# Spread VectorE sums, last store on ScalarE, and first products over three row tiles in a one-core MLP kernel

## The chip, the cores and the metric

The kernel runs on one core of one Trainium2 chip. The metric is the device time of one execution in microseconds (us), lower is better. Most kernels were timed in 3 to 9 executions; their medians are quoted. The spread within such a group is 0.3 to 1.7 us, which is as large as the effects discussed here. So the trace of one profiled execution per kernel, whose times are printed to 0.01 us, carries most of the argument, and the medians are used as a check. One trace is one execution, and its start varies: where this matters, all traces of a kind are given.

Names of engines in profile lines: PE is TensorE (matmul), PEld its weight loads, DVE is VectorE, ACT is ScalarE, POOL is GpSimd, SP is SyncE. An engine's name with q is its sequencer, which issues DMAs.

## The reference

```python
# x: 16 x 512 x 768, w1: 768 x 3072, b1: 3072, w2: 3072 x 768, all float32
y = np.matmul(x, w1) + b1
y = 0.5 * y * (1.0 + erf(y / np.sqrt(2.0)))
return np.matmul(y, w2).astype(np.float32)
```

## The kernel before

The 8192 rows go through in blocks of 1024. Both products are done by a Strassen-Winograd scheme: seven products of half-size operands instead of eight, at the price of sums of operands on VectorE (`x_sums` for x, `prep_wt` for a tile of W1) and sums of results. Operands are float16, sums in PSUM are float32. W1 comes in 12 tiles of 256 columns. The first two row blocks share the W1 tiles (units are the pairs of row block and W1 tile listed in `seq`).

The start, before the Strassen units: SyncE loads row tiles 0 to 3 of x (128 rows each) and W1 tile 0 as float32, VectorE casts them, TensorE transposes x, and W1 tiles 0 and 1 are multiplied with the first row block in the plain way. GpSimd loads W1 tile 1, row tiles 4 to 7 and further W1 tiles meanwhile. `spin` is dummy products, meant to keep TensorE's clock up.

```python
for t in range(4):
    nc.sync.dma_start(out=xf[:, t, :], in_=xr[:, t, :])
for half in range(2):
    r = slice(half * KQ, (half + 1) * KQ)
    nc.sync.dma_start(out=wf[:, r, :], in_=w1r[:, r, 0:2 * P])
# ... (identities, GpSimd's loads)
spin(9)
for t in range(4):
    xhs[t] = xh_of(0, t)
    nc.vector.tensor_copy(out=xhs[t], in_=xf[:, t, :])
    transpose_pe(0, t, copy_halves if t == 3 else nc.scalar.copy)
    # ... (b1 transposed at t == 0)
    spin(2)
for r, c in ((slice(0, KQ), slice(0, P)), (slice(0, KQ), slice(P, 2 * P)),
             (slice(KQ, 2 * KQ), slice(0, 2 * P))):
    nc.vector.tensor_copy(out=w1_raw(wts[0])[:, r, c], in_=wf[:, r, c])
# ...
for half in range(2):
    for side in range(2):
        plain(0, 0, side, half)      # W1 tile 0, rows 0 to 511
for side in range(2):
    plain_done(0, 0, side)
plain(1, 0, 0, 0)                    # W1 tile 1
transpose_pe(0, 4)
# ...
```

The sums of the first units. `fill_a(pos, slot)` is called between the products of unit `pos`; `soon` is a list of VectorE work that is done a little at each slot and emptied at the end of a unit. Unit 7 (`at[1, 0]`) is the first on the second row block.

```python
def fill_a(pos, slot):
    # ...
    if pos == at[1, 0] - 2 and slot in (2, 5):
        transpose_pe(1, X1_PE[slot // 3])
    if slot == (1 if pos < at[1, 0] else 4) and pos + 1 < len(seq) and seq[pos + 1][0] == 0:
        prep_wt(seq[pos + 1][1])           # four sums
    if slot == 4:
        if pos in (3, 6):
            prep_wt(pos // 6)              # W1 tiles 0 and 1 for the second block
        # ...
    if slot == 1:
        if pos in (at[1, 0] - 2, at[1, 0] - 1):
            h = pos - at[1, 0] + 2
            x_sums(1, soon, slice(h * RH // 2, (h + 1) * RH // 2))   # four sums
    # ...
```

The end: the last unit stores a 384 KB block (`u.store(0)`), then finishes the last two 128-row pieces one by one (`last`).

```python
def last(self, banks):
    for t in range(2):
        self.mm(4, banks[t], True, 0, self.C, (t,))
        o = self.dst[:, 1, t, 0, :]
        tt(o, banks[t][:, t * N4:(t + 1) * N4], o, ADD)
        nc.sync.dma_start(out=orr[:, self.sb * 8 + 2 + t, N2:N2 + N4], in_=o)
```

## Time and profile before

| what | value |
|---|---|
| time | 853.23 us, median of 3 (853.05 to 853.4) |
| profiled span | 851.5 us |
| TensorE busy | 844.9 us, 99% |
| VectorE busy | 667.0 us, 78% |

TensorE is the limit: a kernel of this kind can only gain where TensorE waits or does dummy work. The list of waits has three lines for it, 2.6 us in all (columns: engine and what it wrote, then the releaser; us in total, times, longest).

```profile
PE bX L738 <- DVE arena L724: 1.2, 1, 1.2
PE bT L311 <- DVE arena L744: 1.2, 2, 0.9
PE bY L386 <- ACT bY L604: 0.2, 1, 0.2
```

Where the time stands at the start is read from the timeline of TensorE (columns: start us, length us, engine, line, operation, output <- input, shape, count; in brackets the idle time before it and what ended it).

```profile
9.01 0.51 PE L311 MATMUL bT<-ident,arena 128*128 128x128 f16 x6 [0.93 <-DVE arena L744]
...
10.09 0.81 PE L760 MATMUL bX<-arena 128*128 128x512 f16 x3
...
12.67 0.81 PE L760 MATMUL bX<-arena 128*128 128x512 f16 x3
13.32 0.50 PE L311 MATMUL bT<-ident,arena 128*128 128x128 f16 x6
```

The line at 9.01 is the transposes of row tile 3. They wait for VectorE's cast of this tile, which starts when the tile has landed:

```profile
8.04 0.91 DVE L744 CAST arena<-arena 128x768 f16<-128x768 f32 x1 [0.96 <-DMA arena<-in_x_dram]
```

At 10.09 the first real product starts; at 12.67 W1 tile 0 is done and tile 1 begins. I call this moment S. At 13.32 row tile 4 is transposed.

The stretch around 40 us, by windows that each hold one unit (columns: window, its length, busy us and number of instructions of PE, PEld, DVE, ACT and POOL, granted clock, share of the DMA engines, GB/s):

```profile
28.32:32.85 4.53, 4.53 (x22) 2.06 (x21) 4.25 (x12) 3.32 (x5) 0.00 (x0) 1.00 1.23 194
32.85:38.05 5.20, 5.20 (x34) 2.72 (x33) 3.57 (x8) 4.00 (x6) 0.00 (x0) 1.00 1.34 194
38.05:42.92 4.87, 4.70 (x25) 2.06 (x22) 4.70 (x11) 4.00 (x6) 0.00 (x0) 1.00 1.11 279
42.92:47.84 4.92, 4.78 (x23) 2.04 (x22) 4.61 (x11) 3.37 (x6) 0.00 (x0) 1.00 1.02 413
```

A unit of 21 products takes 4.53 us when nothing disturbs it. The second line holds two sets of six transposes, 0.34 us each, so it is not late. The third and fourth are late by 0.34 and 0.39 us, with VectorE busy nearly throughout.

The chain of waits says where the lateness came from (start us, length us, what; the lines left out are issue times and more work of VectorE):

```profile
13.25 11.00 DMA arena<-in_x_dram
...
24.53 11.75 DMA arena<-in_w_dram
...
36.31 0.37 DVE arena L191
...
46.46 0.69 DVE arena L611
...
47.19 0.81 PE bY L386 x3
```

Up to 47 us the kernel was paced by a chain of GpSimd's loads that ends with W1 tile 6 landing at 36.28 (24.53 + 11.75), then by VectorE's backlog from there.

### The profile page before, as it was taken

The numbers are of one execution on the slowest core, as the hardware profiler recorded it, in microseconds if no ns is written. First come the engines' busy times: TensorE is split into PE (matmuls) and PEld (weight loads), VectorE is DVE, ScalarE is ACT, GpSimd is POOL, SyncE is SP. The second block draws the span as 40 slices with busy tenths as digits, with TensorE's granted clock in tenths as the row PEclk, the third lists the DMA queues.
The fourth block names the chain that finished last, engine by engine and source line by source line (L and its number), as shares of the span: only waits on it lengthen the run. The fifth ranks groups of instructions, "written<-read, shape, count | busy, mean of one in ns | idle before, by whom it ended". The sixth has DMA issues, their size and how long they took to land.

```text
span 851.5 us, 16488 instructions
## 1 busy us (share of the span) xinstructions
PE 844.9 (99%) x6432; PEld 568.8 (67%) x6432; DVE 667.0 (78%) x1128; ACT 420.9 (49%) x686; POOL 83.3 (10%) x135
## 2 busy tenths in 40 slices
PE   8999999999999999999999999999999999999998
PEld 5444445687544897448974499645995469944798
DVE  4866678786657998579976799668996689956998
ACT  4777762122277512784138722477216771267611
POOL 5021100002100002000020000200002100010000
PEclk9999999999999999999999999999999999999999
DMA  9996986749999599987999689994999969984398
GB/s 227 213 256 89 253 169 244 267 184 221 212 340 226 186 326 372 304 183 233 334 368 292 141 283 335 360 294 113 312 335 355 277 128 325 347 322 172 100 298 295
DMA packets 143522, 219.05 MB, mean 257 GB/s; under 512 B 61756, under 2 KB 84724, under 8 KB 143444
## 3 DMA queue, kind: packets, MB, share of 16 engines
q1 hardware_dynamic: 117968, 179.83, 66.8%
q0 software_dynamic: 25440, 38.15, 20.7%
q8 instruction: 50, 0.82, 0.4%
q14 instruction: 28, 0.23, 0.1%
q10 hardware_dynamic: 36, 0.01, 0.0%
HBM read 180.30 MB, written 47.87 MB: 268 GB/s over the span
## 4 chain that ended last, share of the span: by engine, by line
PE 94%; DMA 4%; DVE 1%; ACT 0%; issue 0%; POOL 0%; DVEq 0%; ACTq 0%
PE bY L386 20%; PE bY L491 15%; PE bX L386 13%; PE bX L491 10%; PE bW L386 7%; PE bZ L386 7%; PE bZ L491 5%; PE bW L491 5%; PE bY L430 5%; DMA arena<-in_x_dram 3%; PE bZ L430 2%; PE bX L430 2%; PE bW L430 2%; DMA arena<-in_w_dram 1%; PE bY L578 1%; DVE arena L191 1%
## 5 line engine op out<-in xcount | busy, mean ns | idle before, releaser
L191 DVE TENSOR_TENSOR arena<-arena 128x1536 f16<-128x1536 f16 (+7 forms) x632 | 402.9, 668 | 7.8 <-DMA arena<-arena 1.6
L386 PEld LDWEIGHTS <-arena 128*128 128x128 f16 x1974 | 192.5, 98 | 224.7 <-issue 1.1
L491 PEld LDWEIGHTS <-arena 128*128 128x128 f16 x3528 | 292.1, 98 | 8.3 <-issue 0.4
L386 PE MATMUL bY<-arena 128*128 128x512 f16 x846 | 214.5, 379 | 0.3 <-ACT bY L604 0.2
L611 DVE TENSOR_TENSOR arena<-bY,arena 128x512 f32<-128x512 f32 (+1 forms) x102 | 69.3, 680 | 126.3 <-PE bY L386 87.6
L491 PE MATMUL bY<-arena 128*128 128x192 f16 x1500 | 138.3, 246 | 0.0
L386 PE MATMUL bX<-arena 128*128 128x512 f16 x564 | 138.2, 379 | 0.0
L604 ACT COPY bY<-bX 128x512 f32<-128x512 f32 (+1 forms) x143 | 78.6, 550 | 119.3 <-DVE arena L540 81.9
L402 ACT ACTIVATE arena<-arena,b1t 128x1024 f16<-128x1024 f32 x94 | 108.0, 1149 | 54.4 <-DVE arena L639 54.4
L624 ACT COPY arena<-bW 128x512 f32<-128x512 f32 (+1 forms) x147 | 81.0, 551 | 91.0 <-PE bW L491 43.9
L491 PE MATMUL bX<-arena 128*128 128x192 f16 x1020 | 93.1, 246 | 0.1
L639 DVE TENSOR_TENSOR arena<-bZ,arena 128x512 f32<-128x512 f32 (+1 forms) x102 | 69.2, 679 | 20.7 <-PE bZ L386 17.9
L386 PE MATMUL bZ<-arena 128*128 128x512 f16 x282 | 76.2, 379 | 0.0
L386 PE MATMUL bW<-arena 128*128 128x512 f16 x282 | 76.2, 379 | 0.0
L430 PEld LDWEIGHTS <-arena 128*128 128x128 f16 x528 | 51.6, 98 | 34.1 <-issue 0.2
L523 POOL DMA_DIRECT2D out_dram<-arena x42 | 30.5, 728 | 404.8 <-DVE arena L635 368.2
L407 ACT ACTIVATE arena<-bX,b1t 128x512 f16<-128x512 f32 x94 | 64.0, 681 | 10.0 <-PE bX L386 10.0
L407 ACT ACTIVATE arena<-bY,b1t 128x512 f16<-128x512 f32 x94 | 63.3, 673 | 0.0
L655 ACT COPY bZ<-bY 128x512 f32<-128x512 f32 (+1 forms) x54 | 29.0, 537 | 65.9 <-DVE arena L639 33.7
L297 POOL DMA_DIRECT2D arena<-in_x_dram x60 | 32.3, 544 | 250.8 <-DMA arena<-arena 141.3
L491 PE MATMUL bZ<-arena 128*128 128x192 f16 x504 | 48.5, 246 | 0.0
L491 PE MATMUL bW<-arena 128*128 128x192 f16 x504 | 48.5, 246 | 0.0
(60 smaller groups left out, 398.9 us busy)
## 6 DMA issues: line engine op xcount, KB each, us to landing
arena<-w2s SPq DMA_DIRECT2D x294, 288.0 KB, 4.6
arena<-w1s SPq DMA_DIRECT2D x72, 672.0 KB, 7.1
out_dram<-arena POOLq DMA_DIRECT2D x42, 384.0 KB, 7.2
w2s<-arena SPq DMA_DIRECT2D x49, 288.0 KB, 3.7
arena<-in_x_dram POOLq DMA_DIRECT2D x60, 192.0 KB, 7.3
w1s<-arena SPq DMA_DIRECT2D x12, 672.0 KB, 6.6
arena<-in_w_dram POOLq DMA_DIRECT2D x17, 384.0 KB, 7.4
out_dram<-arena SPq DMA_DIRECT2D x17, 384.0 KB, 3.3
```

The lines of the kernel that those rows point to most:

```text
L191: nc.vector.tensor_tensor(out=o, in0=a, in1=b, op=op)
L297: nc.gpsimd.dma_start(out=xhs[t], in_=xr[:, sb * 8 + t, :])
L386: nc.tensor.matmul(out=dst[:, 0:RH], lhsT=w1_op(self.wt, slot)[:, c, :], rhs=a[:, c, :], start=first and c == 0, stop=c == self.C - 1, ski ...
L402: nc.scalar.activation(out=self.G[1][:, hi, :, :], in_=self.tmp, func=GELU, bias=b1t[:, 2 * hi + 1:2 * hi + 2])
L407: nc.scalar.activation(out=self.G[0][:, hi, row, :], in_=bank[:, 0:RH], func=GELU, bias=b1t[:, 2 * hi:2 * hi + 1])
L430: nc.tensor.matmul(out=dst[:, 0:N2], lhsT=a, rhs=w[:, :, c, :], start=first and c == 0, stop=c == self.C - 1, skip_group_check=True)
L491: nc.tensor.matmul(out=dst[:, t * N4:(t + 1) * N4], lhsT=a, rhs=w[:, c, :], start=first and c == 0 and t == ts[0], stop=c == NQ - 1, skip_ ...
L523: eng.dma_start(out=orr[:, s0:s0 + 2, right * N2:(right + 1) * N2], in_=self.dst[:, r].rearrange("p t h n -> p t (h n)"))
L604: nc.scalar.copy(out=bY[u.g % 2][:, 0:u.F], in_=bX[u.g % 2][:, 0:u.F])
L611: nc.vector.tensor_tensor(out=u.c22(), in0=bY[u.g % 2][:, 0:u.F], in1=w[:, 0:u.F], op=ADD)
L624: nc.scalar.copy(out=w[:, 0:u.F], in_=bW[:, 0:u.F])
L639: nc.vector.tensor_tensor(out=u.c12(), in0=bZ[:, 0:u.F], in1=w[:, 0:u.F], op=ADD)
```

## The change: intent and diff

Three parts. First, take VectorE's sums out of the crowded units 5 to 7: three of the four sums of W1 tiles 0 and 1 are done in idle time near the start, and the second x block's sums and second transpose are spread over more units. Second, let ScalarE issue the last store so that it needn't queue behind SyncE's issue. Third, start the products earlier: load W1 tile 0 ahead of row tile 3, multiply the first three row tiles, and do row tile 3 afterwards.

```diff
-        def prep_wt(n):
+        def prep_wt(n, ks=()):
             o = {s: w1_op(wts[n], s) for s in range(7)}
-            for d, a, b in ((T3, B22, T1), (T1, T1, B11), (T2, B22, T1), (T4, B21, T2)):
-                later(KQ * P, lambda d=d, a=a, b=b: tt(o[d], o[a], o[b], SUB), soon)
+            early = ((T3, B22, T1, SUB), (T2, T3, B11, ADD), (T4, B21, T2, SUB), (T1, T1, B11, SUB))
+            usual = ((T3, B22, T1, SUB), (T1, T1, B11, SUB), (T2, B22, T1, SUB), (T4, B21, T2, SUB))
+            for d, a, b, op in [early[k] for k in ks] if ks else usual:
+                later(KQ * P, lambda d=d, a=a, b=b, op=op: tt(o[d], o[a], o[b], op), soon)
@@ the last stores
-                    nc.sync.dma_start(out=orr[:, self.sb * 8 + 2 + t, N2:N2 + N4], in_=o)
+                    (nc.sync, nc.scalar)[t].dma_start(out=orr[:, self.sb * 8 + 2 + t, N2:N2 + N4], in_=o)
@@ the start
-        for t in range(4):
+        for t in range(3):
             nc.sync.dma_start(out=xf[:, t, :], in_=xr[:, t, :])
         ...
             nc.sync.dma_start(out=wf[:, r, :], in_=w1r[:, r, 0:2 * P])
+        nc.sync.dma_start(out=xf[:, 3, :], in_=xr[:, 3, :])
@@
-        for t in range(4):
+        for t in range(3):
             xhs[t] = xh_of(0, t)
             nc.vector.tensor_copy(out=xhs[t], in_=xf[:, t, :])
-            transpose_pe(0, t, copy_halves if t == 3 else nc.scalar.copy)
+            transpose_pe(0, t)
             ...
-            spin(2)
+            spin((2, 2, 4)[t])
@@
+        first, rest = slice(0, 3 * P), slice(3 * P, RH)
+        plain(0, 0, 0, 0, first)
+        plain(0, 0, 1, 0, first)
+        xhs[3] = xh_of(0, 3)
+        nc.vector.tensor_copy(out=xhs[3], in_=xf[:, 3, :])
+        transpose_pe(0, 3, nc.vector.tensor_copy)
+        plain(0, 0, 0, 1, first)
+        plain(0, 0, 1, 1, first)
+        prep_wt(0, range(3))
+        flush(soon)
         for half in range(2):
             for side in range(2):
-                plain(0, 0, side, half)
+                plain(0, 0, side, half, rest)
         for side in range(2):
             plain_done(0, 0, side)
+        prep_wt(1, range(3))
+        flush(soon)
@@ fill_a: second transpose, x sums, W1 sums
+        X1_AT = ((5, 2), (6, 1))
-            if pos == at[1, 0] - 2 and slot in (2, 5):
-                transpose_pe(1, X1_PE[slot // 3])
+            if (pos, slot) in X1_AT:
+                transpose_pe(1, X1_PE[X1_AT.index((pos, slot))])
+            if pos == at[1, 0] - 1 and slot == 2:
+                x_sums(1, soon, slice(RH // 2, RH), (0, 1))
-                if pos in (3, 6):
-                    prep_wt(pos // 6)
+                if pos in (3, 4):
+                    prep_wt(pos - 3, (3,))
-                if pos in (at[1, 0] - 2, at[1, 0] - 1):
-                    h = pos - at[1, 0] + 2
-                    x_sums(1, soon, slice(h * RH // 2, (h + 1) * RH // 2))
+                if pos == at[1, 0] - 2:
+                    x_sums(1, soon, slice(0, RH // 2), (0, 1))
+                if pos == at[1, 0]:
+                    x_sums(1, soon, ks=(2, 3))
... (W1 tiles are stored back to DRAM at earlier units, table KEEP)
```

More of the change, by code (lines that the diff above doesn't have):

```diff
@@ L303, in transpose_dma @@
             nc.sync.dma_start_transpose(out=xT_of(sb, t), in_=xhs[t])
-        def copy_halves(out, in_):
-            for c in (slice(0, KQ), slice(KQ, 2 * KQ)):
-                nc.scalar.copy(out=out[:, c, :], in_=in_[:, c, :])
         def transpose_pe(sb, t, copy=nc.scalar.copy):
@@ L839 @@
         X1_PE = (3, 7)
+        X1_AT = ((5, 2), (6, 1))
+        KEEP = {at[1, 0]: range(7), at[0, 7] + 1: (7,), at[0, 8]: (8,), at[0, 9]: (9,), at[0, 10]: (10,), at[0, 11]: (11,)}
         def transposes_a(pos):
@@ L881, in fill_a @@
                     transposes_a(pos)
-                for n in {at[1, 0]: (0, 2, 3, 4, 6, 5), at[1, 1]: (1,)}.get(
-                        pos, seq[pos][1:] if pos > at[1, 6] and seq[pos][0] and seq[pos][1] > 6 else ()):
+                for n in KEEP.get(pos, ()):
                     keep(n)
```

## The prediction

> What bounds the kernel now. The page gives TensorE 844.9 of 851.5 us busy (99%), the chain of waits is 94% TensorE, and the list of waits has 2.6 us for it in all. In the steady first phase a unit of 21 matmuls of 512 columns takes 4.53 us, 216 ns each. So only three places can give anything: the start, a stretch about 40 us in, and the tail.
>
> 1. Start. The timeline has the first real product at 10.09 us. It waits for row tile 3: landed at 8.0, cast until 8.95, transposed from 9.01, copied by ScalarE from 9.56. W1 tile 0 lands at about 9.1 and 10.1. From 10.09 to 12.67 TensorE runs tile 0's twelve products without a gap. With the change W1's first half should land near 7.8, so six 384-column products start near 8.5 (row tile 2 is copied at 8.49) and last 1 us. Then TensorE, in order, waits for row tile 3, now the last of the same six transfers: landing 9.7 to 10.1, cast 0.56, transposes 0.34, second-half products 0.97, the 128-column rest 0.65: end at 12.3 to 12.7 against 12.67. The 1.6 us won at the first product is mostly given back as a wait for row tile 3. It is capped too: row tiles 4, 5, 6 land at about 12.9, 13.9, 14.9 (DMA view) and are transposed at 13.32, 14.30, 15.29, so a gain over 0.4 us would turn into waits there. Splitting costs little: the Trainium skill ("TensorE: Matmul & The Clock Gate", Part 1) gives a matmul N columns at 2.4 GHz plus about 2.5 ns; the trace agrees (216 ns for 512, 56 for 128), so twelve more cost 0.03 us. The same page lets the clock fall only after about 3.4 us idle; the idle 0.93 us at 8.1 to 9.0 did not lower it here. I expect -0.25 us (0 to -0.4).
>
> 2. Sums. In the windows, the units at 38.70 and 43.57 last 4.87 and 4.92 us, 0.34 and 0.39 over 4.53, with VectorE busy 4.70 and 4.71: sums of W1 tiles 0, 1 and 6 and of the second x block fall on three units, and VectorE starts them late, waiting until 36.31 for W1 tile 6. The 5.20 us of the unit at 33.50 are two transposes (2 x 0.34), which stay. The change puts six W1 sums (0.37 each) into idle VectorE time at 10.7 to 14.9, two into earlier units, and two big x sums one unit later. I count about 4.4, 2.9 and 3.8 us of VectorE then, all under 4.53; the second transposed copy (0.80 on ScalarE) moves too. I expect -0.65 us of the 0.73. The stores of W1 tiles move earlier; TensorE waits in neither place: 0.
>
> 3. Tail. The last VectorE sum ends near 848.27; SyncE issues the two last stores back to back, 847.97 to 848.97, about 0.5 us each. On ScalarE the second can start at 848.3: -0.15 us.
>
> Sum: 853.23 - 0.25 - 0.65 - 0.15 = 852.2 us; range 851.6 to 853.0. Chances: faster by over 2% 0, within 2% 0.99, slower 0.01.
>
> What would show it: first product near 8.5, then a wait of about 1 us at row tile 3's transposes, row tile 4's transposes at 12.95 to 13.3; units near 38 and 43 at 4.53 (4.87 with a transpose); last store issued 0.2 us earlier; TensorE unchanged between.
>
> What would make it wrong: row tile 3 landing after 10.2; W1 tile 1 landing late, with its sums now before VectorE's transposed copies; the wait for W1 tile 6 still pushing VectorE behind.

## The result, and the profile after

The change measured 852.75 us (median of 6, 852.64 to 853.0) against 853.16 us (median of 6, 853.0 to 853.53) of the kernel before in the same rounds. The ratio is 0.9995 with a 95% interval of 0.9982 to 1.0008. Ratios here and below are the mean time of one kernel's fast runs over that of the other's of the same rounds, so not quite the ratio of the medians quoted. The time lies in the predicted range, but the gain is about 0.4 us, not 1.05, so the parts have to be looked at one by one.

TensorE's timeline of the start, after the change:

```profile
8.96 0.66 PE L759 MATMUL bX<-arena 128*128 128x384 f16 x3 [0.77 <-DVE arena L751]
9.46 0.65 PE L759 MATMUL bY<-arena 128*128 128x384 f16 x3
11.00 0.51 PE L309 MATMUL bT<-ident,arena 128*128 128x128 f16 x6 [0.88 <-DVE arena L773]
11.34 0.65 PE L759 MATMUL bX<-arena 128*128 128x384 f16 x3
...
12.99 0.81 PE L759 MATMUL bX<-arena 128*128 128x512 f16 x3
13.63 0.50 PE L309 MATMUL bT<-ident,arena 128*128 128x128 f16 x6
```

The first product starts 1.13 us earlier than before (8.96 against 10.09). After six products TensorE then waits for the cast of row tile 3 (the wait of 0.88 us at 11.00):

```profile
10.38 0.56 DVE L773 CAST arena<-arena 128x768 f16<-128x768 f32 x1 [0.37 <-DMA arena<-in_x_dram]
```

W1 tile 1 begins at S = 12.99, which is 0.32 us later than before.

The units around 40 us, again one window for each:

```profile
33.16:38.03 4.87, 4.87 (x28) 2.39 (x27) 3.38 (x9) 4.00 (x6) 0.00 (x0) 1.00 1.63 182
38.03:43.04 5.01, 5.01 (x28) 2.39 (x27) 3.62 (x8) 4.00 (x6) 0.00 (x0) 1.00 0.99 225
43.04:47.57 4.53, 4.53 (x22) 2.05 (x21) 3.74 (x7) 3.43 (x6) 0.00 (x0) 1.00 1.01 418
```

Two units now hold one set of transposes each, so 4.87 is undisturbed for them. What is left is 0.14 us in the second of these; VectorE is down from 4.7 and 4.6 us to 3.6 and 3.7.

The chain of waits now runs through row tile 3 and then stays on TensorE:

```profile
3.14 7.22 DMA arena<-in_x_dram
10.38 0.57 DVE arena L773
11.00 0.51 PE bT L309 x6
11.51 0.49 PE bX L759 x3
```

The GpSimd loads and VectorE's backlog have left the chain; the load of row tile 3 has come onto it.

The tail. First the issues of the last stores on SyncE, before and then after, with ScalarE's one after:

```profile
847.50 0.37 SPq L523 DMA_DIRECT2D out_dram<-arena  x1
847.97 1.00 SPq L502 DMA_DIRECT2D out_dram<-arena  x2
```

```profile
847.20 0.37 SPq L521 DMA_DIRECT2D out_dram<-arena  x1
847.66 0.44 SPq L500 DMA_DIRECT2D out_dram<-arena  x1
847.99 0.38 ACTq L500 DMA_DIRECT2D out_dram<-arena  x1
```

TensorE ends at E = 847.88 before and 847.57 after (end of the last entry on TensorE in the chain). The last issue is over 1.09 us after E before the change (848.97), and 0.80 us after E with it (848.37). So the issue did come 0.3 us earlier. The span does not show it: the end comes 3.61 us after E before (851.487) and 3.66 us after E with the change (851.232). Pages print spans to 0.1 us only; here and below they are taken from the traces, which hold them to 0.001 us.

With a fourth mark, the start M of the six products on the tile bX with which TensorE goes over to unit 8 (47.84 before, 47.57 after), the span splits into four stretches. This table is used for all experiments; its entries are differences of times read from the traces.

| kernel | S | S to M | M to E | E to end |
|---|---|---|---|---|
| before | 12.67 | 35.17 | 800.04 | 3.61 |
| after | 12.99 | 34.58 | 800.00 | 3.66 |
| difference | +0.32 | -0.59 | -0.04 | +0.05 |

The sum is -0.26 us, the difference of the two profiled spans. So the sums gave what was hoped, the new start cost, and the tail gave nothing. M to E is 799.9 to 800.1 us in every kernel, which bounds what the moved stores of the W1 tiles can have done there. They were not undone alone; before M they are not needed, since the x sums without them (below) reach the lowest S to M that any trace shows.

### The profile page after: what moved, and what is told of

Its sections match the earlier page's. It is cut to its first block, busy times and chain, and to the rows that moved or that the text cites. A ratio compares the mean times of both kernels' runs of the same rounds, so it can differ in the third digit from the quotient of the medians.

```text
span 851.2 us, 16509 instructions
## 1 busy us (share of the span) xinstructions
PE 844.6 (99%) x6444; PEld 569.6 (67%) x6444; DVE 667.6 (78%) x1127; ACT 419.9 (49%) x684; POOL 83.4 (10%) x135
## 4 chain that ended last, share of the span: by engine, by line
PE 98%; DMA 1%; SPq 0%; DVE 0%; issue 0%
PE bY L384 21%; PE bY L489 15%; PE bX L384 14%; PE bX L489 10%; PE bZ L384 7%; PE bW L384 7%; PE bZ L489 5%; PE bW L489 5%; PE bY L428 5%; PE bZ L428 2%; PE bX L428 2%; PE bW L428 2%; PE bY L576 1%; DMA arena<-in_x_dram 1%; PE bX L576 1%; PE bX L759 0%
## 5 line engine op out<-in xcount | busy, mean ns | idle before, releaser
L191 DVE TENSOR_TENSOR arena<-arena 128x768 f16<-128x768 f16 (+4 forms) x630 | 403.4, 671 | 8.0 <-DMA arena<-arena 2.0
L609 DVE TENSOR_TENSOR arena<-bY,arena 128x512 f32<-128x512 f32 (+1 forms) x102 | 69.4, 681 | 127.1 <-PE bY L384 89.4
```

Of the source, the lines that this page charges most:

```text
L191: nc.vector.tensor_tensor(out=o, in0=a, in1=b, op=op)
L609: nc.vector.tensor_tensor(out=u.c22(), in0=bY[u.g % 2][:, 0:u.F], in1=w[:, 0:u.F], op=ADD)
```

## The experiments

Twelve kernels in three sets. The kernels of a set ran on one chip and share runs of the kernel before. The medians of before were 853.42, 853.23 and 853.15 us.

### The three parts alone

**New start alone.** The kernel before with the load order and the first products of the change, without the early sums:

```diff
-        for t in range(4):
+        for t in range(3):
             nc.sync.dma_start(out=xf[:, t, :], in_=xr[:, t, :])
         ...
+        nc.sync.dma_start(out=xf[:, 3, :], in_=xr[:, 3, :])
... (loop over three tiles, spin and products as in the change's diff)
```

> The kernel before with only the new start (W1 tile 0 ahead of row tile 3, first products over three row tiles). Theory: TensorE in order waits for row tile 3, which is now the last of six transfers; with the landing of about 10.4 us of the after trace, tile 0 ends near 13.0 instead of 12.7, so this is 0.2 to 0.3 us slower than before (853.4). Rival (the recorded prediction): 0.25 us faster (852.9).

Measured: 853.88 us (5 runs) against 853.42, ratio 1.0006 (0.9993 to 1.0018). S is 13.93, the latest of all: in this execution row tile 2 was cast only from 8.14 us (6.52 before), and all that follows it came late. S to M is 34.79 and E comes 0.78 us after that of before, though S is 1.26 us later: part of the late start was absorbed by the waits that this kernel still has in the middle. The interval holds 1, so the time alone proves no loss; the sign in trace and time is the theory's.

**Sums alone.** The change with start and last store put back:

```diff
-        nc.sync.dma_start(out=xf[:, 3, :], in_=xr[:, 3, :])   # after W1, as the change had it
+        ... (the old start: four row tiles, then W1, then plain(0, 0, side, half))
         prep_wt(0, range(3)); flush(soon)   # both stay, now behind all of tile 0's products
         prep_wt(1, range(3)); flush(soon)
-                    (nc.sync, nc.scalar)[t].dma_start(...)
+                    nc.sync.dma_start(...)
```

> The kernel before with only the spread sums (and the moved stores of W1 tiles), old start, old last store. Theory: the two units near 38.7 and 43.6 us lose their 0.34 and 0.39 us, so about 0.6 us faster (852.55). Rival: the sums give only about 0.4 us, the whole measured gain, and start and tail are both neutral.

Measured: 852.69 us (5 runs) against 853.42, ratio 0.9993 (0.9979 to 1.0007). In the trace S is 12.70, S to M 34.45, E to end 3.60. The whole excess of the middle is gone: 35.17 less 34.45 is 0.72 us, and E is 0.59 us earlier than before.

**Last store alone.**

```diff
-                    nc.sync.dma_start(out=orr[:, self.sb * 8 + 2 + t, N2:N2 + N4], in_=o)
+                    (nc.sync, nc.scalar)[t].dma_start(out=orr[:, self.sb * 8 + 2 + t, N2:N2 + N4], in_=o)
```

> The kernel before with only the last store on ScalarE. Theory: from 847 to 850 us the DMA engines are fully busy with stores that were already queued, so an earlier issue of the last store gives 0 to 0.1 us (853.1). Rival (the recorded prediction): 0.15 us faster or more (853.0).

Measured: 853.26 us (5 runs) against 853.42, ratio 0.9999 (0.9987 to 1.0012). E to end is 3.66 us against 3.61 before. The part gives nothing. Its trace also shows how start and middle hang together: S was 12.21 by chance, 0.46 us earlier than in the trace of before, but S to M grew to 35.30.

**The change without the new start** (sums and last store):

```diff
-        for t in range(3):
+        for t in range(4):
... (old start as in the sums alone; the last store stays on ScalarE)
```

> The changed kernel with the old start put back. Theory: it beats the changed kernel by what the new start costs, 0.2 to 0.3 us, so about 852.5. Rival: it is 0.25 us slower than the changed kernel (853.0).

Measured: 852.81 us (5 runs; one of them 854.31) against 853.42, ratio 0.9998 (0.9985 to 1.001). S is 12.53, S to M 34.57, E to end 3.67. E is 847.19 against 847.57 of the change, which agrees with the theory by trace, but the medians (852.81 here, 852.75 for the change) do not show it, and they are from different rounds. The time leaves this point open, and the traces are one execution each: with the old start S is 12.17 to 12.70 in six traces, with the new one 12.48 to 12.99 in six and 13.93 in the new start alone. So the new start is later on the whole, but the ranges overlap.

### The start again

**The change once more**, unaltered.

> The changed kernel once more, unaltered, for direct comparison on one chip and for a second profile of its start. Theory: the first products of W1 tile 1 (the end of tile 0) begin at 12.9 to 13.9 us, against 12.2 to 12.7 in the four profiles with the old start; the two units near 38 and 43 us have no wait; time about 0.4 us under before. Rival (the recorded prediction): the first trace had a bad start by chance and this one shows tile 0 ended before 12.6 us.

Measured: 852.81 us (5 runs) against 853.23, ratio 0.9994 (0.9982 to 1.0007). S is 12.94, S to M 34.44: the late start came again, and the 0.14 us left in the middle of the first trace did not. So the middle of the changed kernel can be free of waits, but isn't in every execution. In the first trace VectorE waits in that unit for a DMA transpose, and its next sum of a product (L609) starts 3.63 us into the unit, here 3.26 us. In a kernel below (old load order, split products) the same sum starts at 3.68 us, and 0.19 us are lost. That fits, but no run tested it.

**GpSimd's loads held back**, on the changed kernel. The Trainium skill ("DMA: Bandwidth & Descriptors", Queues, rings and completion order) says that each DMA engine takes turns between the queues that have work for it, packet by packet. So GpSimd's loads might slow row tile 3's transfer.

```diff
-        nc.gpsimd.tensor_copy(out=xh_of(0, 4)[:, 0:1], in_=xf[:, 0, 0:1])
+        nc.gpsimd.tensor_copy(out=xh_of(0, 4)[:, 0:1], in_=xf[:, 2, 0:1])
```

> The changed kernel with GpSimd's loads (W1 tile 1 and row tiles 4 on) held back until row tile 2 has landed instead of row tile 0, about 2 us later. Theory: those loads share the DMA engines with row tile 3's transfer from about 8.5 us; held back, row tile 3 lands at 9.6 to 9.9 instead of 10.38 and tile 0 ends 0.4 us or more earlier, after which TensorE waits for W1 tile 1 and the whole is slower. Rival: row tile 3 is late only because five transfers go before it; it lands at 10.2 or later all the same.

Measured (one run, state unknown): 853.31 us. VectorE's casts of the last three loads, in VectorE's timeline:

```profile
8.21 0.75 DVE L751 CAST arena<-arena 128x384 f16<-128x384 f32 x2 [0.81 <-DMA arena<-in_w_dram]
9.27 0.60 DVE L751 CAST arena<-arena 128x768 f16<-128x768 f32 x1 [0.31 <-DMA arena<-in_w_dram]
10.23 0.70 DVE L773 CAST arena<-arena 128x768 f16<-128x768 f32 x1 [0.36 <-DMA arena<-in_x_dram]
```

Row tile 3 is cast from 10.23, against 10.25 and 10.38 in the two profiles of the change. The earlier landing that the theory of contention expected did not come. But the run is a weak test of it. The loads were issued 2.7 us later (7.38 against 4.67), yet the packets of GpSimd's queue begin at 9.06 against 8.80 in the first trace of the change: in both, SyncE's queue has the DMA engines to itself until then. From 8.5 to 10.0 us GpSimd's queue moves about 75 KB here and 162 KB there, so the overlap with row tile 3 was halved and not removed. Whether the engines take turns packet by packet is not shown, and a small cost of it stays possible. What the traces do show is the rival: from 4.0 to 8.5 us SyncE's own transfers fill the engines (share 1.02, 351 GB/s), and row tile 3 is the last of them. S is 12.98, without a wait for W1 tile 1, which surprised me; the hold-back was paid later, with VectorE waiting for W1 tile 6 until 37.21 instead of 36.52, and S to M at 34.93.

**Old load order, split products**, on the sums alone. Row tile 3 keeps its place ahead of W1, but TensorE doesn't wait for it before the first products:

```diff
-        for half in range(2):
-            for side in range(2):
-                plain(0, 0, side, half)
+        first, rest = slice(0, 3 * P), slice(3 * P, RH)
+        for r in (first, rest):
+            for side in range(2):
+                plain(0, 0, side, 0, r)
+        for side in range(2):
+            plain(0, 0, side, 1)
...
-            spin(2)
+            spin((2, 2, 2, 1)[t])
```

> The spread sums with the old load order (row tile 3 before W1), the old last store, but the products of W1's first half over three row tiles before those of row tile 3. Theory: nothing waits for a later transfer, TensorE starts at W1's first half (about 9.7 us) instead of 10.09, tile 0 ends near 12.3 us, and the run is 0.1 to 0.3 us faster than the changed kernel by start alone plus about 0.3 us, so near 852.4. Rival: the start is bound by the landings of W1 tile 1 and row tile 4 (12.0 to 13.2 us), so this equals the spread sums alone (852.7).

Measured: 852.62 us (5 runs) against 853.23, ratio 0.9992 (0.9978 to 1.0005). In TensorE's timeline:

```profile
9.59 0.66 PE L762 MATMUL bX<-arena 128*128 128x384 f16 x3 [0.21 <-DVE arena L754]
...
12.27 0.81 PE L762 MATMUL bX<-arena 128*128 128x512 f16 x3
13.15 0.49 PE L313 MATMUL bT<-ident,arena 128*128 128x128 f16 x6
```

S is 12.27, as expected, and 0.67 us earlier than the changed kernel on the same chip. But three products of 512 columns take 0.65 us, so row tile 4's transposes could have started at 12.92 and start at 13.15: 0.23 us are lost to the landing of row tile 4. S to M is 34.86, and E is 847.25 against 847.36 of the change on that chip and 847.29 of the sums alone. The other 0.19 us are lost in the unit from 37.54 to 42.60, which takes 5.06 us instead of 4.87. Theory and rival were each half right: the start itself is better, and about half of what it wins is held up by the next load.

### The two halves of the sums

**x sums and second transpose alone**, on the kernel before:

```diff
+        X1_AT = ((5, 2), (6, 1))
-            if pos == at[1, 0] - 2 and slot in (2, 5):
-                transpose_pe(1, X1_PE[slot // 3])
+            if (pos, slot) in X1_AT:
+                transpose_pe(1, X1_PE[X1_AT.index((pos, slot))])
+            if pos == at[1, 0] - 1 and slot == 2:
+                x_sums(1, soon, slice(RH // 2, RH), (0, 1))
... (x_sums at slot 1 of units 5 and 7 as in the change; prep_wt stays)
```

> The kernel before with only the sums of the second x block split and moved, and its second transpose one unit later; the sums of W1 tiles 0 and 1 stay at their old places. Theory: one of the two waits goes, the one near 43.6 us (0.39 us) whose VectorE time falls; the middle (first product of W1 tile 1 to the end of TensorE) is 834.8 to 834.9 us against 835.21 before and 834.58 with all parts. Rival: this part alone takes away all of it (834.6).

**Sums of W1 tiles 0 and 1 alone**, on the kernel before:

```diff
... (prep_wt with ks, as in the change)
+        prep_wt(0, range(3)); flush(soon)
+        prep_wt(1, range(3)); flush(soon)
-                if pos in (3, 6):
-                    prep_wt(pos // 6)
+                if pos in (3, 4):
+                    prep_wt(pos - 3, (3,))
```

> The kernel before with only the sums of W1 tiles 0 and 1 made early; the x sums, the transposes and the W1 stores stay as before. Theory: 0.2 to 0.4 us of the 0.63 goes: the middle is 834.8 to 835.0 us; both parts are needed. Rival: this part alone takes away all of it (834.6), or nothing (835.2).

Measured: the x sums 852.57 us (4 runs) against 853.15, ratio 0.9994 (0.9979 to 1.0009); the W1 sums 852.88 us (4 runs), ratio 0.9998 (0.9983 to 1.0013). The units in question, x sums alone:

```profile
37.21:42.08 4.87, 4.87 (x28) 2.39 (x27) 3.87 (x8) 4.10 (x7) 0.00 (x0) 1.00 1.17 275
42.08:46.61 4.53, 4.53 (x22) 2.06 (x21) 4.43 (x9) 3.27 (x5) 0.00 (x0) 1.00 1.02 413
```

and W1 sums alone:

```profile
37.59:42.38 4.79, 4.69 (x24) 2.05 (x22) 4.69 (x10) 3.96 (x6) 0.00 (x0) 1.00 0.92 214
42.38:47.00 4.62, 4.62 (x22) 2.04 (x21) 3.83 (x7) 3.75 (x6) 0.00 (x0) 1.00 1.03 427
```

In its trace the first takes away all of it: 4.87 is a unit with a transpose, 4.53 one without, and S to M is 34.44. VectorE is still busy 4.43 of 4.53 us in the second of these units and TensorE does not care. The second leaves 0.26 and 0.09 us, S to M 34.79. By these traces the rival of the first expectation was right: the x sums with the moved transpose suffice, and the six early W1 sums add slack, not time. Both were started from a good start (S 12.17 and 12.21), so E and the medians may not be set against each other without S.

### The tail

My theory for the tail was a backlog of stores: the DMA engines are fully busy from 845 us on. These windows are after the change (columns as above):

```profile
845.50:847.50 2.00, 2.00 (x26) 1.83 (x23) 1.84 (x4) 0.00 (x0) 0.00 (x0) 1.00 1.02 361
847.50:849.50 2.00, 0.06 (x1) 0.00 (x0) 0.36 (x1) 0.00 (x0) 0.00 (x0) 1.00 0.99 335
849.50:850.00 0.50, 0.00 (x0) 0.00 (x0) 0.00 (x0) 0.00 (x0) 0.00 (x0) 1.00 0.65 200
```

The last column but one is the share of the engines. It stays near 1 until the last bytes leave at about 849.83, which is 2.26 us after E. Read in steps of 0.1 us, this figure is 2.2 to 2.3 us in before, change, last store alone and sums alone, whoever issues the last store.

**One earlier store left out** (wrong: a 384 KB part of the output is not written, issued near 843 us), on the changed kernel:

```diff
                 tt(par[3][:, r], par[2][:, r], par[3][:, r], ADD)
-                self.store(r)
+                if self.sb + 1 < nsb or r == 0:
+                    self.store(r)
```

> Wrong on purpose: the changed kernel without one of the last stores of 384 KB (one half of the lower right block of the last 1024 rows, issued near 843 us). Theory: the DMA engines work off a backlog of stores after the last matmul; without that store they are idle earlier and the time from the end of TensorE to the end falls from 3.6 us by 0.5 to 1.0 us, so the last store's issue was not what ended last. Rival: the tail is set by the last store's own issue and landing; the 3.6 us stay within 0.1.

Measured: 853.0 us (4 runs) against 853.23; E to end 3.70 us. The backlog is gone, and the end has not moved:

```profile
847.50:848.00 0.50, 0.02 (x1) 0.00 (x0) 0.36 (x1) 0.00 (x0) 0.00 (x0) 1.00 0.37 121
848.00:848.50 0.50, 0.00 (x0) 0.00 (x0) 0.00 (x0) 0.00 (x0) 0.00 (x0) 1.00 0.89 319
848.50:849.00 0.50, 0.00 (x0) 0.00 (x0) 0.00 (x0) 0.00 (x0) 0.00 (x0) 1.00 1.04 381
849.00:849.50 0.50, 0.00 (x0) 0.00 (x0) 0.00 (x0) 0.00 (x0) 0.00 (x0) 1.00 1.00 318
849.50:850.00 0.50, 0.00 (x0) 0.00 (x0) 0.00 (x0) 0.00 (x0) 0.00 (x0) 1.00 0.52 161
```

The engines are idle most of the half microsecond before 848 and still finish at 849.75. So the theory of a backlog from earlier stores falls. From 848 on they carry the 384 KB store issued at 847.15 and the two last ones of 96 KB. That is 0.59 MB; at the 0.35 MB per us of the two full half microseconds (381 and 318 GB/s) it takes about 1.7 us (an estimate from these numbers), which is what is seen. The next two runs test that.

**The 384 KB store before the last two left out** (also wrong), with the last store on ScalarE, and the same with it on SyncE:

```diff
                 if u.ends:
-                    u.store(0)
+                    pass
```

> Wrong on purpose: the changed kernel without the 384 KB store that is issued 0.5 us before the two last ones. Theory: it is this store's bytes behind which the last two wait; without it the DMA engines go idle 1.5 to 1.8 us after the end of TensorE instead of 2.26, and the run ends 0.4 to 0.7 us earlier. Rival: the last bytes still leave at 2.26.

> Wrong on purpose: the same without that store, but both last stores on SyncE as before the change. Theory: now that nothing hides the issue, the second store on SyncE starts late, and the DMA engines go idle 0.2 to 0.4 us later (counted from the end of TensorE) than with ScalarE: the move is worth what was predicted only where no bytes are queued ahead. Rival: no difference, so that the issue of the last store never matters.

Measured: 851.84 us (ScalarE) and 852.12 us (SyncE), 4 runs each, against 853.15. E to end falls to 3.06 and 3.01 us, and the last bytes leave 1.7 us after E in both (about 848.67 less 846.96, and 848.45 less 846.80). So it is that store's bytes behind which the last two wait. The issues of the last two, first with ScalarE (SyncE has issued the other from 846.87), then both on SyncE:

```profile
847.37 0.38 ACTq L500 DMA_DIRECT2D out_dram<-arena  x1
```

```profile
846.72 0.84 SPq L500 DMA_DIRECT2D out_dram<-arena  x2
```

The second expectation fell: even with that store gone, ScalarE's issue is no better. In this kernel SyncE, not having just issued another store, has both issues done in 0.84 us, at 847.56, which is 0.76 us after E; ScalarE's was done 0.79 us after E (847.75 less 846.96). The second store waits for VectorE's last sum, not for the sequencer.

## Why the prediction was right or wrong

The time was right (852.75 in 851.6 to 853.0, predicted 852.2), and of its three terms one was. That the time was right is in part luck, or the width of the range: it held gains from about 0.2 to 1.6 us, so one right term was enough, while the two others had the wrong sign.

- **What bounds the kernel.** Right. From M to E all traces take the same time within 0.3 us.
- **Sums, predicted -0.65 us.** Right: -0.59 in the first trace of the change, -0.73 in the second (35.17 less 34.44), -0.72 with the sums alone. The reason was partly off. I credited the six early W1 sums as well; the x sums and the moved transpose do it all by themselves. The feared wait for W1 tile 6 remained in some executions. In the first trace of the change VectorE waits until 36.52 and TensorE's chain doesn't show it; with one earlier store left out, a change far away at 843 us, it waits until 36.86, the chain runs from that load into TensorE, and S to M is 34.65.
- **Start, predicted -0.25 us (0 to -0.4).** Wrong in sign: +0.32 in the first trace, +0.27 in the second (against the one trace of before, from other rounds). The structure was right: early first products, then a wait for row tile 3 in order. The step that failed is "landing 9.7 to 10.1, cast 0.56, transposes 0.34, second-half products 0.97, the 128-column rest 0.65: end at 12.3 to 12.7". Row tile 3 was cast only from 10.38 and 10.25, and from there to S it took 2.61 and 2.69 us, not 2.52. I had taken the six landings of before and permuted them; W1's first half, put at 7.8, came at 8.40 and about 8.28. In the third set, where row tile 3 was cast from 9.81 and 9.71, S was 12.63 and 12.48, inside my range, but the old start was at 12.17 and 12.21 there: what hastens the landings hastens both starts. The new order puts the load with the long tail (cast, transposes, copy, products) last; the old one ends with W1's second half, which needs a cast only. In the first trace the cast of row tile 3 begins 2.34 us later than before (10.38 against 8.04), and what follows it until S is only 2.02 us shorter (2.61 against 4.63): that is the 0.32.
- **The cap on the start.** Right, and it applies to the better start too: with S at 12.27, row tile 4's transposes waited 0.23 us.
- **What I did not say about start and sums.** In the kernel before, the chain of waits up to 47 us lay on GpSimd's loads and VectorE, not on TensorE's start. So the terms don't simply add: a start 1.26 us later cost 0.78 us there, and a start 0.46 us earlier gave 0.35 us at E (847.53 against 847.88).
- **Tail, predicted -0.15 us.** Wrong in sign: about +0.05 (E to end is 3.66 to 3.70 us in six traces with ScalarE, 3.59 to 3.61 in six with SyncE; the same 0.05 in the two kernels without the 384 KB store). Why it ends a little later with ScalarE stays open. The step that failed is "On ScalarE the second can start at 848.3: -0.15 us". The issue did move by 0.3 us, but the bytes of the 384 KB store issued 0.5 us earlier hold the engines. "Trainium Kernel Development and Optimization" (Key Constraints) of the Trainium skill says that DMAs from the several queues share the 16 engines, and that issuing from several engines "only saves the sequencer's issue time". The runs agree as far as they go: the issue time was saved, and the end came no earlier. I had costed a sequencer and not the engines behind it.
- **Cost of splitting, and the clock.** Right. The Trainium skill ("TensorE: Matmul & The Clock Gate", Part 1) makes a matmul N columns at 2.4 GHz plus about 2.5 ns; in the changed kernel six products of 384 columns go from 11.34 to 12.32, 163 ns each, and twelve of 128 columns from 12.32 to 12.99, 56 ns each. The 0.88 us of waiting before 11.00 did not slow those products, which fits the page's statement that the clock falls after about 3.4 us idle.

What stays open: whether the sums alone are faster than the whole change by more than the noise. The traces say 0.1 to 0.3 us (E 847.29 against 847.57 and 847.36, with E to end alike within 0.06). The medians do not settle it: 852.69 for the sums alone, 852.81 for the sums with the last store, both with the old start, against 852.75 and 852.81 for the change, from different sets. Only the old load order with split products ran beside the change (852.62 against 852.81), and the ratios of the two to before overlap. The best against before by ratio is the old load order with split products (852.62 us, 0.9992); its interval, like all the others, still holds 1.

## What to carry to other kernels

When an in-order engine is given early work from loads that came first, ask what follows the load that now comes last: a transfer with a cast, a transpose, a copy and products behind it belongs ahead of one that needs a cast only. Before speeding up the issue of a last store, look at whether the DMA engines are already full of the store ahead of it; if they are, bytes count and issue time does not. And where a chain of loads paces a stretch, a better start and a better middle do not add up: undo each part alone and split the span at marks on the busiest engine, because a few tenths of a microsecond could not be seen in these medians.

## What the Trainium skill lacked or had wrong

- No page gives the spread of landing times of the first loads from run to run. With the same first three transfers, VectorE began to cast row tile 2 at 6.16 us in one profile and at 8.14 in another, and S moved with the landings that follow; belongs to "DMA: Bandwidth & Descriptors".
- "DMA: Bandwidth & Descriptors" (Queues, rings and completion order) tells how queues take turns, but not that a queue's loads, once issued, can move nothing for microseconds while another queue fills the engines: GpSimd's loads, issued from 4.67 us, have their first packet at 8.80, and issued from 7.38 us they have it at 9.06. What held them is not shown.
- The sentence on issue time in "Trainium Kernel Development and Optimization" held, but neither it nor the DMA page says that at the end of a kernel issue time is hidden while bytes are queued: a last issue 0.3 us earlier left the last bytes at 2.26 us after E, taking 384 KB away brought the end forward by 0.6 us.
